# Loading the modulation matrix first, the small parameters from ScalarE's queue, and the front's projection weights through a pool of their own

## The chip, the cores and the metric

The kernel runs on one core of a Trainium2 chip. Its engines are TensorE (PE; PEld is its weight load), VectorE (DVE), ScalarE (ACT), GpSimd (POOL) and SyncE (SP). Each works through its own instructions in the order in which they stand. Copies between device memory and on-chip memory are issued by an engine's sequencer (SP in most cases, ACT and POOL in some) and carried by 16 DMA engines. The metric is the device time of one execution in microseconds.

## The reference

One layer of a hybrid backbone over 2048 latent tokens and 256 context tokens, all in 32-bit floats. What matters here is its beginning:

```python
silu_c, silu_cc = silu(c), silu(c_ctx)
mod_l = silu_c @ ada_w + ada_b              # 1024 -> 6 * 1024: shift, scale, gates
mod_c = silu_cc @ ada_w + ada_b
hl = rms_norm(x, norm_mix_pre) * (1 + scale_l) + shift_l
hc = rms_norm(ctx, norm_mix_pre) * (1 + scale_c) + shift_c
p = hl @ w_in, hc @ w_in                    # columns split among three mixers
...                                         # RWKV-7, gated delta net, RG-LRU in both directions
x = x + gate * rms_norm(concat(mixers) @ w_out)
x = x + gate * rms_norm(square(relu(h2 @ ffn_up)) @ ffn_down)
```

No product with `w_in` can start before scale and shift are known, and these need `c`, `c_ctx`, the first 2048 columns of `ada_w` (8 MB) and a part of `ada_b`.

## The kernel before

`body` runs four stages: `front`, `mixed`, `rest`, `ffn`. Only `front` is touched. Tokens go through it in nine pieces of 256, the context first.

- `K.__init__` makes constants on GpSimd and calls `params`. It loads 19 small vectors, row by row, into two tiles of 128 rows (`rawA`: c, c_ctx, ada_b and two norms; `rawB`: the rest) with 21 transfers from SP (lines 182 and 187), transposes each tile on TensorE and copies it to `parA`, `parB`.
- `ada_first` computes silu(c) as `cs` (two tanh on ScalarE into `csth`, four small VectorE steps), loads the 8 MB of `ada_w` as four tiles `adawt` of 2 MB (two transfers each, line 216) and multiplies: per tile 8 products (`adps`, recorded as 16 matmuls), a copy `adar`, four small transposes `adpt`, two additions. The result is `sc` and `sh`.
- `make_h` is a generator. It writes zeros between the pieces of the scratch tensor `ht` (`zf`, three transfers of 2048 runs of two or three numbers, line 295), loads a piece of x as two tiles `mhx`, takes sums of squares on ScalarE, runs `rms` (a chain of small VectorE steps), scales on GpSimd, then transposes (`mhps`), applies `sc` and `sh` (ScalarE for one half of the split numbers, VectorE for the other, in tiles `mhh`) and writes to `ht`, four transfers of 512 KB for a piece.
- `Proj` holds `w_in` as high and low parts (`whi`, `wlo`): `weight` loads 256 KB pieces into a staging buffer, ScalarE casts the high part, VectorE or GpSimd subtracts. The staging buffers are the six `hx` units, which later hold pieces read back from `ht` (four units a piece).
- `rwkv_sweep` multiplies piece by piece (`proj`) and does the RWKV preparation, and advances `make_h` beside it.

The order within each engine is set by a scheduler that goes by its own model of time when the program is built. Transfers issued by SP and ACT count on eight semaphores (DMAHW0 to 7) in turn. An issue waits until the transfer that used its semaphore before has landed, so eight at most are in flight from both engines together; and as each engine works in order, what stands behind a waiting issue waits too. Buffers given out again make their new writer wait for the last reader.

Of the kernel before, what the change touches and what calls it, by code (L numbers as in the profile page):

```python
# [7 lines left out]
F32 = mybir.dt.float32  # L8
# [4 lines left out]
PSUM = bass.MemoryType.PSUM  # L13
DRAM = bass.MemoryType.DRAM
ADD, SUB, MUL = ALU.add, ALU.subtract, ALU.mult

D = 1024
KD = 8
# [12 lines left out]
C_Z, C_BA, C_LX, C_LG, C_RW = 1152, 1536, 1560, 1816, 2072  # L31
# [44 lines left out]
class K:  # L76


    def __init__(self, tc, d, es):
        self.tc, self.nc, self.d = tc, tc.nc, d  # L80
        nc = self.nc
        self.V, self.A, self.G, self.PE, self.S = nc.vector, nc.scalar, nc.gpsimd, nc.tensor, nc.sync
        self.const = es.enter_context(tc.tile_pool(name="const", bufs=1))
        self.cols = {}
        self.tables = self.section = None
        self.inside = []
        c = self.const
        self.ident = c.tile([128, 128], F32, name="ident")
        self.G.memset(self.ident, 0.0)
        self.G.affine_select(self.ident, self.ident, pattern=[[-1, 128]], compare_op=ALU.not_equal,  # L90
                             fill=1.0, base=0, channel_multiplier=1)
        self.ones2 = c.tile([128, 128], F32, name="ones2")
        self.G.memset(self.ones2, 0.0)
        self.G.memset(self.ones2[0:64, 0:64], 1.0)
        self.G.memset(self.ones2[64:128, 64:128], 1.0)
        self.ones = c.tile([128, 128], F32, name="ones")
        self.G.memset(self.ones, 1.0)
        self.params()

    def col(self, v):  # L100

# [61 lines left out]

    def params(self):

        d, S, tc = self.d, self.S, self.tc
        rowsA = [("c", 8), ("c_ctx", 8), ("ada_b", 48), ("norm_mix_pre", 8), ("norm_ffn_pre", 8)]
        rowsB = [("gdn_conv", 36), ("lru_conv", 8), ("lru_conv_b", 2), ("lru_ba", 4), ("lru_bx", 4),
                 ("lru_lambda", 4), ("rwkv_mu", 12), ("rwkv_w0", 6), ("rwkv_a0", 6), ("rwkv_k_k", 3),
                 ("rwkv_k_a", 3), ("rwkv_r_k", 3), ("rwkv_gn_w", 3), ("rwkv_gn_b", 3)]  # L170
        self.pc = {}
        with tc.tile_pool(name="par", bufs=1) as p, tc.tile_pool(name="parp", bufs=2, space=PSUM) as pp:
            for nm, rows in (("A", rowsA), ("B", rowsB)):
                n = sum(r for _, r in rows) + (1 if nm == "B" else 0)
                raw = p.tile([128, 128], F32, name=f"raw{nm}")
                self.G.memset(raw, 0.0)
                o = 0
                place = {}
                for k, r in rows:
                    src = d[k]  # L180
                    names = " ".join(f"a{i}" for i in range(len(src.shape)))
                    S.dma_start(out=raw[o:o + r, :], in_=src.rearrange(f"{names} -> ({names})").rearrange("(r q) -> r q", q=128))
                    place[k] = (o, r)
                    o += r
                if nm == "B":
                    for hh in range(2):
                        S.dma_start(out=raw[o:o + 1, 64 * hh:64 * hh + 64], in_=d["gdn_norm"])
                    place["gdn_norm"] = (o, 1)
                ps = pp.tile([128, 128], F32, name=f"parps{nm}")
                self.PE.transpose(ps, raw, self.ident)  # L190
                t = self.const.tile([128, 128], F32, name=f"par{nm}")
                self.V.tensor_copy(t, ps)
                for k, (o, r) in place.items():
                    self.pc[k] = t[:, o:o + r]

def ada_first(k, pp, tag):

    c = k.const  # L200
    k.cs = c.tile([128, 2, KD], F32, name="cs")
    th = c.tile([128, 2, KD], F32, name="csth")
    for j, nm in enumerate(("c", "c_ctx")):
        k.act(th[:, j], k.pc[nm], AF.Tanh, scale=0.5)
        k.ts(k.V, th[:, j], th[:, j], 0.5, MUL, 0.5, ADD)
        k.tt(k.V, k.cs[:, j], th[:, j], k.pc[nm], MUL)
    k.sc = c.tile([128, 2, KD], F32, name="sc")
    k.sh = c.tile([128, 2, KD], F32, name="sh")
    with k.tc.tile_pool(name="adaw", bufs=4, reuse_waits="tile") as p:
        for j, o in ((1, k.sc), (0, k.sh)):  # L210
            for hf in range(2):
                w = p.tile([128, KD, 512], F32, name="adawt")
                c0 = j * D + hf * 512
                for q in range(2):
                    s = slice(4 * q, 4 * q + 4)
                    k.S.dma_start(out=w[:, s, :], in_=k.d["ada_w"][0, 512 * q:512 * q + 512, c0:c0 + 512].rearrange(
                        "(k p) f -> p k f", p=128))
                ps = pp.tile([128, 512], F32, name="adps", tag=tag)
                for kk in range(KD):
                    k.mm(ps[0:2, :], k.cs[:, :, kk], w[:, kk, :], kk == 0, kk == KD - 1)  # L220
                row = p.tile([2, 512], F32, name="adar", bufs=1)
                k.V.tensor_copy(row, ps[0:2, :])
                ps = pp.tile([128, 4, 2], F32, name="adpt", tag=tag)
                for m in range(4):
                    k.PE.transpose(ps[:, m, :], row[:, 128 * m:128 * m + 128], k.ident[0:2, 0:2])
                m = slice(4 * hf, 4 * hf + 4)
                for i in range(2):
                    k.tt(k.V, o[:, i, m], ps[:, :, i], k.pc["ada_b"][:, 8 * j + m.start:8 * j + m.stop], ADD)
    for i in range(2):
        k.stt(k.sc[:, i], k.sc[:, i], 1.0, k.pc["norm_mix_pre"], ADD, MUL)  # L230

# [55 lines left out]
def make_h(k, w, pp, tag):  # L287


    d = k.d  # L290
# [3 lines left out]
    for o, n in ((0, 2), (258, 3), (2309, 3)):  # L294
        k.S.dma_start(out=ht[:, :, o:o + n], in_=zf[:, :, 0:n])

    def load(p):
        xt = []
        for i in range(2):
            t = w.tile([128, D], F32, name="mhx", bufs=2)  # L300
            src = d["ctx"][0, 128 * i:128 * i + 128, :] if p == 0 else \
                d["x"][0, 256 * (p - 1) + 128 * i:256 * (p - 1) + 128 * i + 128, :]
            k.S.dma_start(out=t, in_=src)
            xt.append(t)
        return xt

    xt = load(H_ORDER[0])
    yield
    for n, p in enumerate(H_ORDER):
        j = 1 if p == 0 else 0  # L310
# [7 lines left out]
        for i, x in enumerate(xt):  # L318
            o = poff(p) + 2 + 128 * i
            for q in range(2):  # L320
                ps = pp.tile([128, 4, 128], F32, name="mhps", tag=tag)
                for a in range(4):
                    kk = 4 * q + a
# [16 lines left out]
def split(k, e, src, raw, hi, lo):  # L340

    k.S.dma_start(out=raw, in_=src)
    k.A.copy(hi, raw)  # L343
    k.tt(e, lo, raw, hi, SUB)
    return hi, lo


class Proj:
# [6 lines left out]
        self.pp = es.enter_context(tc.tile_pool(name=tag + "p", bufs=psb, space=PSUM, side=side))  # L355
        self.nw = 0

    def weight(self, i, c0, m):

        k = self.k  # L360
        self.hi[i], self.lo[i] = [self.w.tile([128, KD, m], F32R, name=f"w{x}{i}") for x in ("hi", "lo")]
        n = 2 * self.u
        for q in range(0, KD, n):
            s = slice(q, q + n)
            split(k, (k.V, k.G)[i % 2], k.d["w_in"][0, 128 * q:128 * (q + n), c0:c0 + m].rearrange("(k p) f -> p k f", p=128),
                  self.unit().bitcast(F32).rearrange("p k a t -> p (k a t)")[:, 0:n * m].rearrange("p (k f) -> p k f", f=m),
                  self.hi[i][:, s, :], self.lo[i][:, s, :])

# [1 line left out]

        return self.hp.tile([128, self.u, 2, PW], F32R, name="hx")

    def weights(self, cols):

        self.hi, self.lo, self.coming = {}, {}, ()
        for i, c in enumerate(cols):
            self.weight(i, *c)

    def passes(self, sets):

# [13 lines left out]
    def load(self, p):  # L394

        out = []
        o = poff(p)
        for q in range(0, KD, self.u):
            x = self.unit()
            self.k.S.dma_start(out=x.bitcast(F32).rearrange("p k a t -> p (k a) t"),  # L400
                               in_=self.k.d["ht"][:, q:q + self.u, :, o:o + PW].rearrange("p k a t -> p (k a) t"))
            out.append(x)
        return out
# [353 lines left out]
RW_TILES = [9, 10, 11, 3, 4, 5, 6, 7, 8, 0, 1, 2]  # L757


def rwkv_sweep(k, pj, pss, beside):  # L760


    d, tc, V, A, G = k.d, k.tc, k.V, k.A, k.G
# [1 line left out]
    with ExitStack() as es:  # L765
# [37 lines left out]
                k.stt(out, ps[:, 0:256], hmu[:, f:f + 1], out, MUL, ADD)  # L803
                k.stt(out, ps[:, 2:258], hmu[:, f:f + 1], out, MUL, ADD)

        ahead = pj.load(RW_ORDER[0])
        for i, p in enumerate(RW_ORDER):
            h = ahead
            if i + 1 < NP:
# [97 lines left out]
def front(k):  # L907

    with ExitStack() as es:
        pj = Proj(k, es, "r", psb=3, u=2, hb=6, side="left")  # L910
        pss = es.enter_context(k.tc.tile_pool(name="rss", bufs=3, space=PSUM))
        parts = make_h(k, es.enter_context(k.tc.tile_pool(name="mh", bufs=1, side="right")), pss, "rps")
        next(parts)
        ada_first(k, pss, "rps")
        for _ in range(9):
            next(parts)
        pj.weights([(C_RW + 128 * f, 128) for f in RW_TILES])
        rwkv_sweep(k, pj, pss, parts)


def softplus(k, p, x, n, m, tag):
# [945 lines left out]
```

## Time and profile before

| | us |
|---|---|
| median of 3 runs (lowest, highest) | 4212.22 (4210.96, 4213.60) |
| the profiled execution's own time | 4211.31 |
| its span on the core | 4209.5 |
| TensorE busy | 3570.4 (85%) |
| VectorE, ScalarE, GpSimd busy | 2391.7, 1480.0, 1387.2 |

The profile's page gives averages over stages with different limits, so for a change at the start the views of the first 110 us are read: the timeline of each engine (with the idle time before an instruction and what ended it), the busy times and DMA rates by stretch, and the waits. PEclk is the granted clock of TensorE (0.5 is 1.2 GHz, 1.0 is 2.4 GHz).

### The profile page before, as it was taken

The page shows a single profiled execution, that of the slowest core. Times are in us where ns is not written, and L with a number is a line of the kernel's source. Part 1 is how long each engine was busy: PE and PEld are TensorE (multiplying, and loading weights), DVE is VectorE, ACT ScalarE, POOL GpSimd, SP SyncE. Part 2 cuts the span into 40 slices and gives each one's busy share as a digit, 9 for nine tenths or more (in the row PEclk, how much of TensorE's full clock was granted, in tenths as well). Part 3 has the DMA queues.
Part 4 walks back from the last instruction along what each step waited for, and adds up shares of the span by engine and source line. Part 5 has one row for each costly group of instructions (what it writes and reads, how often), then busy time and mean ns, then how long its engine had stood idle before and what let it go on. Part 6 is the DMA issues. An engine that isn't in the chain of part 4 may idle for free. (4 is left out here: it accounts for less than half of the span.)

```text
span 4209.5 us, 75439 instructions
## 1 busy us (share of the span) xinstructions
PE 3570.4 (85%) x29914; PEld 2983.6 (71%) x29914; DVE 2391.7 (57%) x4533; ACT 1480.0 (35%) x2983; POOL 1387.2 (33%) x1373
## 2 busy tenths in 40 slices
PE   4767798688878876788787589989999999999998
PEld 1646678587767766677665467768888887888886
DVE  3456576885686562359979975643333346333334
ACT  2343344344445432223454444532222222211212
POOL 2123123233434432225456545322232214212212
PEclk8868899688979877688897679999999999999999
DMA  8554443656657755375665555631212123111112
GB/s 209 114 134 138 118 150 136 187 155 182 199 175 219 224 170 164 111 225 167 189 210 160 158 174 177 204 116 46 66 57 62 56 73 126 55 46 46 53 43 85
DMA packets 568885, 566.07 MB, mean 134 GB/s; under 512 B 42179, under 2 KB 521044, under 8 KB 568532
## 3 DMA queue, kind: packets, MB, share of 16 engines
q1 hardware_dynamic: 554708, 538.16, 42.9%
q0 software_dynamic: 5120, 16.78, 1.4%
q10 hardware_dynamic: 8704, 6.29, 0.5%
q8 instruction: 237, 3.88, 0.4%
q14 instruction: 116, 0.95, 0.1%
HBM read 425.96 MB, written 145.77 MB: 136 GB/s over the span
## 5 line engine op out<-in xcount | busy, mean ns | idle before, releaser
L162 PE MATMUL proj<-hx,whi 128*128 128x258 f32 (+2 forms) x4080 | 865.4, 309 | 99.5 <-DMA hx<-ht 40.9
L162 PEld LDWEIGHTS proj<-hx,whi 128*128 128x128 f32 x4080 | 684.9, 203 | 145.7 <-issue 66.9
L162 PE MATMUL proj<-hx,wlo 128*128 128x258 f32 (+2 forms) x2040 | 616.6, 303 | 0.0
L136 DVE TENSOR_TENSOR facc<-facc,fdn 128x512 f32<-128x512 f32 x480 | 326.1, 686 | 401.3 <-PE fdn L162 401.3
L162 PEld LDWEIGHTS proj<-hx,wlo 128*128 128x128 f32 x2040 | 413.2, 203 | 11.3 <-issue 6.8
L162 PE MATMUL fup<-fhh,uhi 128*128 128x512 f32 x1024 | 403.9, 395 | 3.8 <-ACT fhh L343 3.8
L162 PE MATMUL fup<-fhl,uhi 128*128 128x512 f32 x1024 | 402.9, 394 | 3.5 <-DVE fhl L136 3.3
L162 PE MATMUL fdn<-dhi,ah 128*128 128x512 f32 x1024 | 399.3, 391 | 4.1 <-ACT ah L1767 2.0
L162 PE MATMUL fup<-fhh,ulo 128*128 128x512 f32 x1024 | 402.8, 393 | 0.0
L162 PE MATMUL fdn<-dlo,ah 128*128 128x512 f32 x1024 | 399.2, 390 | 0.2 <-POOL dlo L136 0.2
L162 PE MATMUL fdn<-dhi,al 128*128 128x512 f32 x1024 | 395.0, 390 | 0.9 <-DVE al L136 0.9
L343 ACT CAST dhi<-draw 128x1024 fp32r<-128x1024 f32 x64 | 67.1, 1048 | 578.9 <-PE fdn L162 514.4
L136 POOL TENSOR_TENSOR dlo<-draw,dhi 128x1024 fp32r<-128x1024 f32 x32 | 77.5, 2421 | 565.0 <-ACT dhi L343 565.0
L136 POOL TENSOR_TENSOR fq<-fr 128x512 f32<-128x512 f32 x128 | 151.7, 1186 | 325.1 <-ACT fr L114 324.4
L162 PEld LDWEIGHTS fup<-fhl,uhi 128*128 128x128 f32 x1024 | 192.5, 188 | 49.1 <-DVE fhl L136 5.0
L162 PEld LDWEIGHTS fup<-fhh,uhi 128*128 128x128 f32 x1024 | 192.5, 188 | 48.8 <-ACT fhh L343 4.9
L162 PEld LDWEIGHTS fdn<-dhi,ah 128*128 128x128 f32 x1024 | 192.1, 188 | 48.6 <-DVE facc L136 3.3
L162 PEld LDWEIGHTS fup<-fhh,ulo 128*128 128x128 f32 x1024 | 192.3, 188 | 44.4
L136 DVE TENSOR_TENSOR al<-fq,ah 128x512 fp32r<-128x512 f32 x128 | 93.6, 732 | 227.3 <-ACT ah L1767 226.9
L162 PEld LDWEIGHTS fdn<-dhi,al 128*128 128x128 f32 x1024 | 192.2, 188 | 42.3 <-DVE al L136 1.3
L162 PEld LDWEIGHTS fdn<-dlo,ah 128*128 128x128 f32 x1024 | 192.3, 188 | 41.8 <-POOL dlo L136 0.6
L144 DVE SCALAR_TENSOR_TENSOR gy<-proj,parB,gy 128x256 f32<-128x256 f32 x243 | 115.1, 479 | 136.2 <-ACT gy L114 132.9
(365 smaller groups left out, 7207.4 us busy)
## 6 DMA issues: line engine op xcount, KB each, us to landing
hx<-ht SPq DMA_DIRECT2D x144, 520.0 KB
hx<-ht SPq DMA_DIRECT2D x36, 1040.0 KB
uraw<-in_ffn_up_dram SPq DMA_DIRECT2D x64, 512.0 KB
draw<-in_ffn_down_dram SPq DMA_DIRECT2D x64, 512.0 KB
pk<-pk SPq DMA_DIRECT2D x18, 1536.0 KB
pk<-pk SPq DMA_DIRECT2D x36, 768.0 KB
ht<-mhh SPq DMA_DIRECT2D x36, 512.0 KB
pb<-pk SPq DMA_DIRECT2D x36, 384.0 KB
```

Source lines behind the costliest of these rows:

```text
L136: return e.tensor_tensor(out=out, in0=a, in1=b, op=op)
L144: return self.V.scalar_tensor_tensor(out=out, in0=a, scalar=s, in1=b, op0=op0, op1=op1)
L162: self.last = self.PE.matmul(out, l, r, start=start, stop=stop).ins
L343: k.A.copy(hi, raw)
```

## The change

`params` is called later and issues from ScalarE's queue, as does the load of the first piece; the eight transfers of `ada_w` are issued by SP ahead of all else; the `w_in` staging gets 24 buffers of its own, which reuse the memory of the `ada_w` tiles; and the loads of `w_in` and of the first piece of `ht` are asked for after the first piece of h.

```diff
     # K.__init__
-        self.params()
     # params
-        d, S, tc = self.d, self.S, self.tc
+        d, S, tc = self.d, self.A, self.tc
-        with ... tc.tile_pool(name="parp", bufs=2, space=PSUM) as pp:
+        with ... tc.tile_pool(name="parp", bufs=1, space=PSUM) as pp:
+ADA_FIRST = ((1, 0), (1, 1), (0, 0), (0, 1))
+def ada_load(k, p):          # the loads, taken out of ada_first as they were
+    for j, hf in ADA_FIRST:
+        w = p.tile([128, KD, 512], F32, name="adawt")
...
     # make_h
-    def load(p):
+    def load(p, q=k.S):
-            k.S.dma_start(out=t, in_=src)
+            q.dma_start(out=t, in_=src)
-    xt = load(H_ORDER[0])
+    xt = load(H_ORDER[0], k.A)
     # Proj.weight
-                  self.unit().bitcast(F32)...
+                  raw.tile([128, n, m], F32, name="wraw") if raw else
+                  self.unit().bitcast(F32)...
     # rwkv_sweep: the first piece is handed in
-        ahead = pj.load(RW_ORDER[0])
     # front
-        next(parts)
-        ada_first(k, pss, "rps")
-        for _ in range(9):
-            next(parts)
-        pj.weights([(C_RW + 128 * f, 128) for f in RW_TILES])
-        rwkv_sweep(k, pj, pss, parts)
+        with k.tc.tile_pool(name="adaw", bufs=4, reuse_waits="tile") as p:
+            ws = ada_load(k, p)
+            k.params()
+            parts = make_h(k, mh, pss, "rps")
+            next(parts)
+            ada_first(k, p, ws, pss, "rps")
+        with k.tc.tile_pool(name="wst", bufs=2 * len(RW_TILES), reuse_waits="tile") as p:
+            for _ in range(3):
+                next(parts)
+            first = pj.load(RW_ORDER[0])
+            pj.weights([(C_RW + 128 * f, 128) for f in RW_TILES], p)
+            for _ in range(6):
+                next(parts)
+        rwkv_sweep(k, pj, pss, parts, first)
```

How ScalarE's instructions stand at the start: before, it has no transfers, and the tanh into `csth` is its fourth instruction.

```order
L129 ACT_TABLE_LOAD
L114 ACTIVATE mhh,mhs<-mhx 128x1024 [waits DMAHW0_49]
L114 ACTIVATE mhh,mhs<-mhx 128x1024 [waits DMAHW1_49]
L114 ACT_TABLE_LOAD
L114 ACTIVATE csth<-parA 128x8 [waits DVE_49]
```

In the changed kernel the same engine issues 23 transfers first; these are the last of them and what follows (each names the semaphore on which it waits).

```order
L181 DMA rawB<-in_rwkv_k_a_dram 3x128 [waits DMAHW3_49]
L181 DMA rawB<-in_rwkv_r_k_dram 3x128 [waits DMAHW4_49]
L181 DMA rawB<-in_rwkv_gn_w_dram 3x128 [waits DMAHW5_49]
L181 DMA rawB<-in_rwkv_gn_b_dram 3x128 [waits DMAHW6_49]
L186 DMA rawB<-in_gdn_norm_dram 1x64 [waits DMAHW7_49]
L186 DMA rawB<-in_gdn_norm_dram 1x64 [waits DMAHW0_49]
L312 DMA mhx<-in_ctx_dram 128x1024 [waits DMAHW1_49]
L113 ACT_TABLE_LOAD
L113 ACTIVATE mhh,mhs<-mhx 128x1024
L128 ACT_TABLE_LOAD
L113 ACT_TABLE_LOAD
L113 ACTIVATE csth<-parA 128x8 [waits DVE_49]
```

The tanh now stands behind all parameter loads, both context tiles and three table loads.

SP's transfers at the start, before: the parameters, the zeros, `ada_w`, `w_in`.

```order
L182 DMA rawB<-in_rwkv_gn_b_dram 3x128
L187 DMA rawB<-in_gdn_norm_dram 1x64 x2
L295 DMA ht<-zf 2048x1x2
L295 DMA ht<-zf 2048x1x3 x2
L216 DMA adawt<-in_ada_w_dram 128x4x512 x8
L342 DMA hx<-in_w_in_dram 128x4x128 x23
```

And in the changed kernel, from the sixth transfer of `ada_w` on, with the semaphores.

```order
L208 DMA adawt<-in_ada_w_dram 128x4x512 [waits DMAHW2_49]
L208 DMA adawt<-in_ada_w_dram 128x4x512 [waits DMAHW4_49]
L208 DMA adawt<-in_ada_w_dram 128x4x512 [waits DMAHW6_49]
L304 DMA ht<-zf 2048x1x2 [waits DMAHW0_49,Pool_49]
L304 DMA ht<-zf 2048x1x3 [waits DMAHW2_49]
L304 DMA ht<-zf 2048x1x3 [waits DMAHW4_49]
L351 DMA wraw<-in_w_in_dram 128x4x128 [waits DMAHW2_49,DMAHW1_49,PE_49]
L351 DMA wraw<-in_w_in_dram 128x4x128 [waits DMAHW3_49,PE_49]
L312 DMA mhx<-in_x_dram 128x1024 [waits DMAHW4_49,PE_49,Pool_49]
L351 DMA wraw<-in_w_in_dram 128x4x128 [waits DMAHW5_49]
```

The zeros moved behind `ada_w`; their semaphores 0, 2 and 4 are those that ScalarE's later parameter loads wait on (`rwkv_r_k`, number 4, above). The third `w_in` transfer stands behind a load of x that waits for TensorE.

SP further on, before: the first piece goes out to `ht` and comes back as `hx` with `w_in` long issued.

```order
L333 DMA ht<-mhh 128x8x128
L303 DMA mhx<-in_x_dram 128x1024
L333 DMA ht<-mhh 128x8x128 x2
L400 DMA hx<-ht 128x4x260 x2
L333 DMA ht<-mhh 128x8x128
L400 DMA hx<-ht 128x4x260 x2
```

In the changed kernel the same stretch, from the third transfer of `w_in` on.

```order
L351 DMA wraw<-in_w_in_dram 128x4x128 x10
L342 DMA ht<-mhh 128x8x128
L312 DMA mhx<-in_x_dram 128x1024
L342 DMA ht<-mhh 128x8x128
L351 DMA wraw<-in_w_in_dram 128x4x128 x12
L342 DMA ht<-mhh 128x8x128 x2
L410 DMA hx<-ht 128x4x260 x2
```

Ten and then twelve of the 24 transfers of `w_in` now stand between the load of x and the last writes of the first piece.

## Rows read from the trace of the kernel before

**Rows 1.** TensorE, timeline: start us, us, engine line op, tiles, [idle before <-releaser]

```profile
26.70 9.41 PE L162 MATMUL adps<-adawt,cs 128*2 128x512 f32 x16 [14.83 <-DMA adawt<-in_ada_w_dram]
...
45.03 0.41 PE L225 MATMUL adpt<-ident,adar 2*128 2x2 f32 x4 [0.77 <-DVE adar L222]
...
63.66 0.41 PE L225 MATMUL adpt<-ident,adar 2*128 2x2 f32 x4 [3.13 <-DVE adar L222]
...
95.09 0.77 PE L162 MATMUL proj<-hx,whi 128*128 128x258 f32 x2 [22.18 <-DMA hx<-ht]
...
104.11 0.51 PE L162 MATMUL proj<-hx,whi 128*128 128x258 f32 x2 [1.49 <-DMA hx<-ht]
```

**Rows 2.** SP's timeline

```profile
0.81 0.87 SPq L303 DMA_DIRECT2D mhx<-in_ctx_dram  x2
...
4.49 0.27 SPq L182 DMA_DIRECT2D rawB<-in_lru_conv_dram  x1
...
9.67 0.54 SPq L187 DMA_DIRECT2D rawB<-in_gdn_norm_dram  x2
10.33 2.78 SPq L295 DMA_DIRECT2D ht<-zf  x3
13.16 20.05 SPq L216 DMA_DIRECT2D adawt<-in_ada_w_dram  x8
33.26 12.09 SPq L342 DMA_DIRECT2D hx<-in_w_in_dram  x6
```

**Rows 3.** by stretch: PE, PEld, DVE, ACT, POOL busy, PEclk, DMA share, GB/s

```profile
16.00:17.00 1.00, 0.00 (x0) 0.00 (x0) 0.00 (x0) 0.00 (x0) 0.00 (x0) 1.00 2.47 7
...
19.00:20.00 1.00, 0.00 (x0) 0.00 (x0) 0.00 (x0) 0.00 (x0) 0.00 (x0) 1.00 1.09 62
...
24.00:25.00 1.00, 0.00 (x0) 0.00 (x0) 0.00 (x0) 0.00 (x0) 0.00 (x0) 1.00 0.71 184
25.00:26.00 1.00, 0.00 (x0) 0.00 (x0) 0.00 (x0) 0.00 (x0) 0.00 (x0) 1.00 1.03 397
```

**Rows 4.** the same view, while ada_w and while w_in are loaded

```profile
36.00:40.00 4.00, 3.23 (x12) 0.92 (x12) 0.91 (x3) 0.00 (x0) 0.00 (x0) 1.00 1.05 409
...
52.00:56.00 4.00, 3.23 (x11) 0.83 (x11) 2.34 (x5) 1.89 (x4) 2.39 (x3) 1.00 1.00 260
```

**Rows 5.** by stretch, later in the front

```profile
150.00:200.00 50.00, 33.93 (x253) 33.57 (x253) 20.48 (x63) 17.57 (x35) 5.70 (x2) 0.79 0.63 135
```

**Rows 6.** TensorE's waits, 95 to 600 us; columns: total us, times, longest

```profile
PE rps L162 <- POOL kd L136: 28.1, 4, 13.9
PE proj L162 <- ACT mhh L114: 23.7, 3, 19.1
```

**Rows 7.** ScalarE's timeline at the start

```profile
4.50 1.06 ACT L114 ACTIVATE mhh<-mhx 128x1024 f32<-128x1024 f32 x1 [2.41 <-DMA mhx<-in_ctx_dram]
...
7.00 1.28 ACT L114 ACT_TABLE_LOAD   x1
8.29 0.31 ACT L114 ACTIVATE csth<-parA 128x8 f32<-128x8 f32 x2
```

**Rows 8.** transfers by kind, 0 to 130 us: count, KB each

```profile
adawt<-in_ada_w_dram SPq DMA_DIRECT2D x8, 1024.0 KB
hx<-in_w_in_dram SPq DMA_DIRECT2D x24, 256.0 KB
ht<-mhh SPq DMA_DIRECT2D x8, 512.0 KB
```

**Rows 9.** SP's waits, 0 to 130 us

```profile
SPq L182 <- DMA mhx<-in_ctx_dram: 1.7, 2, 1.0
```

**Rows 10.** the rms chain before the second piece: VectorE's first step

```profile
92.04 0.15 DVE L141 TENSOR_SCALAR rms<-mhs 128x1 f32<-128x1 f32 x1 [3.88 <-ACT mhh L114]
```

**Rows 11.** and GpSimd, which waits for its end

```profile
94.86 5.67 POOL L140 TENSOR_SCALAR mhx<-mhx,rms 128x1024 f32<-128x1024 f32 x2 [22.97 <-DVE rms L144]
```

**Rows 12.** SP, the first piece out to ht and back

```profile
90.85 0.91 SPq L400 DMA_DIRECT2D hx<-ht  x2
```

More of the change, by code (lines that the diff above doesn't have):

```diff
@@ L171, in params @@
         self.pc = {}
-        with tc.tile_pool(name="par", bufs=1) as p, tc.tile_pool(name="parp", bufs=2, space=PSUM) as pp:
+        with tc.tile_pool(name="par", bufs=1) as p, tc.tile_pool(name="parp", bufs=1, space=PSUM) as pp:
             for nm, rows in (("A", rowsA), ("B", rowsB)):
@@ L194, in params, with ada_first @@
                     self.pc[k] = t[:, o:o + r]
-def ada_first(k, pp, tag):
+ADA_FIRST = ((1, 0), (1, 1), (0, 0), (0, 1))
+def ada_load(k, p):
+    ws = []
+    for j, hf in ADA_FIRST:
+        w = p.tile([128, KD, 512], F32, name="adawt")
+        c0 = j * D + hf * 512
+        for q in range(2):
+            s = slice(4 * q, 4 * q + 4)
+            k.S.dma_start(out=w[:, s, :], in_=k.d["ada_w"][0, 512 * q:512 * q + 512, c0:c0 + 512].rearrange(
+                "(k p) f -> p k f", p=128))
+        ws.append(w)
+    return ws
+def ada_first(k, p, ws, pp, tag):
     c = k.const
@@ L208, in ada_first @@
     k.sh = c.tile([128, 2, KD], F32, name="sh")
[L209 to L228, printed above, removed]
+    for (j, hf), w in zip(ADA_FIRST, ws):
+        o = k.sc if j else k.sh
+        ps = pp.tile([128, 512], F32, name="adps", tag=tag)
+        for kk in range(KD):
+            k.mm(ps[0:2, :], k.cs[:, :, kk], w[:, kk, :], kk == 0, kk == KD - 1)
+        row = p.tile([2, 512], F32, name="adar", bufs=1)
+        k.V.tensor_copy(row, ps[0:2, :])
+        ps = pp.tile([128, 4, 2], F32, name="adpt", tag=tag)
+        for m in range(4):
+            k.PE.transpose(ps[:, m, :], row[:, 128 * m:128 * m + 128], k.ident[0:2, 0:2])
+        m = slice(4 * hf, 4 * hf + 4)
+        for i in range(2):
+            k.tt(k.V, o[:, i, m], ps[:, :, i], k.pc["ada_b"][:, 8 * j + m.start:8 * j + m.stop], ADD)
     for i in range(2):
@@ L356, in __init__, with weight @@
         self.nw = 0
-    def weight(self, i, c0, m):
+    def weight(self, i, c0, m, raw=None):
         k = self.k
@@ L371, in unit, with weights @@
         return self.hp.tile([128, self.u, 2, PW], F32R, name="hx")
-    def weights(self, cols):
+    def weights(self, cols, raw=None):
         self.hi, self.lo, self.coming = {}, {}, ()
         for i, c in enumerate(cols):
-            self.weight(i, *c)
+            self.weight(i, *c, raw)
     def passes(self, sets):
@@ L757, with rwkv_sweep @@
 RW_TILES = [9, 10, 11, 3, 4, 5, 6, 7, 8, 0, 1, 2]
-def rwkv_sweep(k, pj, pss, beside):
+def rwkv_sweep(k, pj, pss, beside, ahead):
     d, tc, V, A, G = k.d, k.tc, k.V, k.A, k.G
@@ L911, in front @@
         pss = es.enter_context(k.tc.tile_pool(name="rss", bufs=3, space=PSUM))
-        parts = make_h(k, es.enter_context(k.tc.tile_pool(name="mh", bufs=1, side="right")), pss, "rps")
-        next(parts)
-        ada_first(k, pss, "rps")
-        for _ in range(9):
-            next(parts)
-        pj.weights([(C_RW + 128 * f, 128) for f in RW_TILES])
-        rwkv_sweep(k, pj, pss, parts)
+        mh = es.enter_context(k.tc.tile_pool(name="mh", bufs=1, side="right"))
+        with k.tc.tile_pool(name="adaw", bufs=4, reuse_waits="tile") as p:
+            ws = ada_load(k, p)
+            k.params()
+            parts = make_h(k, mh, pss, "rps")
+            next(parts)
+            ada_first(k, p, ws, pss, "rps")
[7 more added lines that the diff above has]
+        rwkv_sweep(k, pj, pss, parts, first)
 def softplus(k, p, x, n, m, tag):
```

## The prediction

> **What bounds the kernel now.** The change touches only the first stage, so I read that stage in order of time. TensorE's timeline comes first: it idles until 26.70 us, when the first tile of `ada_w` is there, works through four tiles until 64.07, and idles again until 95.09, when the first piece has come back from `ht` [rows 1]. Next, SP's timeline says why `ada_w` is late: ahead of it stand the parameters, until 10.21, and three transfers of zeros; the 8 MB go out from 13.16 [rows 2]. The view by stretch prices the zeros: from about 11 to 25 us the DMA engines are busy and move almost nothing, 7 GB/s at 16 us and still 184 at 24, and only from 25 on do they reach 397 [rows 3]. While `ada_w` runs alone it is 409 GB/s; while `w_in` runs it is 260 at a full DMA share [rows 4]. The reader should see a chain: zeros, `ada_w`, TensorE's four tiles, the first piece out and back. After it TensorE is busy 33.9 of 50 us and waits for the other engines [rows 5, 6].
>
> **The change, part by part.**
>
> *`ada_w` first.* Its issue moves from 13.16 to 0.81 us [rows 2]. With the flow starting near 2 us (an estimate from that issue and the first use of a context tile at 4.50 [rows 7]), 8.39 MB [rows 8] and one context tile of 0.52 MB take 8.91 / 0.409 = 21.8 us [rows 4] and are in by 24. Taken alone that would let TensorE start long before 26.70.
>
> *The zeros behind it.* They are issued as soon as the fifth to seventh transfers land, and stand in the same queue behind the eighth. Before, `ada_w` got nothing done until the zeros were through [rows 3], so I take the queue as first in, first out here too: 24 + 13 = 37 us. Lower bound for the 13 is 8 (the first bytes of `ada_w` pass at 19 us, 62 GB/s), upper 14.
>
> *Parameters on ScalarE's queue.* Here the change works against itself. An issue waits for the transfer that had its semaphore before: SP's load of `lru_conv` stood until 4.49, held by a context tile [rows 2, 9]. In the new order `rwkv_r_k` waits on semaphore 4, last used by the third transfer of zeros, hence until 37. Behind it ScalarE still has six issues at 0.3 us each [rows 2], the second context tile's among them: 1.9, to 39. Then a table load, 1.28, and the sum of squares, 1.06 + 0.19 for its readout, rounded to 1.2 [rows 7]. VectorE must run the whole `rms` chain before it reaches the copy of `parA`, on which the tanh waits: 94.86 − 92.04 = 2.8 [rows 10, 11], during which two more table loads pass on ScalarE. Copy 0.3 (an estimate, two small steps), tanh 0.3 [rows 7], and four small steps for `cs` that I put at 0.9 (0.15 each [rows 10] with gaps): 6.8 together. The first product starts at 39 + 6.8 = 46, not 26.70: 19 us later. Before, `cs` had long been ready and its cost was nothing, because the wait for `ada_w` hid it; that cover is gone.
>
> No row shows ScalarE waiting at an issue of its own. The Trainium skill ("DMA: Bandwidth & Descriptors", Anatomy of one DMA) states that the DMA engines never wait on semaphores; the wait sits on the issuing sequencer before dispatch. By that rule ScalarE stands still as SP does; were it otherwise, the first rival below would hold.
>
> *TensorE's four tiles.* From 26.70 to 64.07 is 37.4 us, of which the last small transposes lost 3.13 − 0.77 = 2.4 to a VectorE that was held by the `w_in` splits [rows 1]. In the new kernel the splits come later, so 35.0. The transposes of `parB` slip in behind the first tile; their loads land about 2 us after 39 and the tile ends near 55, so that costs nothing. Modulation is done at 46 + 35 = 81 instead of 64.07: **+17**.
>
> *`w_in` behind the first piece.* Its first two transfers wait only for TensorE to be done with the tiles whose memory they reuse. The third stands on SP behind a load of x that waits for the context tile to be transposed, that is, until just after modulation. So 22 of 24 transfers, which before were hidden beside the four tiles (26 to 64 us), now share the next stretch with the first piece. From modulation to the first product of the sweep was 95.09 − 64.07 = 31.0 us [rows 1]. Now it must pass 22 × 0.262 MB of `w_in` and four writes of 0.524 MB at 260 GB/s, (5.77 + 2.10) / 0.260 = 30.2, and two loads of x, 1.05 / 0.409 = 2.6 [rows 4, 8]; then the reading back, 95.09 − 90.85 = 4.2 [rows 1, 12]. With 0.5 for the first transposes that is 37.5, or 6.5 more. The second half of the piece gives some back: it arrived 9.0 us after the first (104.11 [rows 1]), held by the last write; now that write is issued ahead of both, so it follows at once and the second half starts about 4 later than before. I take **+5**. Lower bound 0 (the loads pass beside ScalarE's and VectorE's work on the piece, which before also left the DMA idle at times), upper +9 (every write queued behind all of `w_in`).
>
> *The rest.* The own staging pool frees the `hx` units, on whose reuse SP waited before; this lay beside the four tiles and is worth nothing. The single buffer for the parameter transposes makes `parB` wait for the copy of `parA`, done long before. After about a sixth of TensorE's and a quarter of VectorE's instructions the order is the same as before, so there is no lasting reorder to price; swaps of stores and loads inside the sweep may move a few us either way.
>
> *Sum.* 17 + 5 = +22 us on the profiled execution's 4211.3 (span 4209.5) gives 4233; the median of the runs shown, 4212.2, is 0.9 above that execution, so nothing changes. I assume the delay passes down whole: behind the first product every wait is for an engine that works on the same pieces [rows 6], and nothing started earlier runs on its own.
>
> A rule that speaks against the whole idea: the Trainium skill ("DMA: Bandwidth & Descriptors", Issuing engines are not separate DMA queues) says that issuing from several engines saves only the sequencer's issue time. SP's parameter issues end at 10.21 [rows 2], so by it the split could save at most some 9 us of issuing, and the trace agrees that the zeros, not the issues, fill the time from 11 to 25.
>
> **Rivals.**
>
> *ScalarE is not held (faster).* If all the semaphores were free in time, 23 issues at 0.3 us would end near 8; plus 6.8 the first product starts at 15, TensorE paces the tiles, modulation ends at 50, 14 early; less the 6.5 for `w_in`: −8, 4203. For it: the early transfers are tiny, and `ada_w` is in time for each tile (2 MB in 5 us against (63.66 − 2.4 − 45.03) / 2 = 8.1 of TensorE a tile [rows 1]). Against: the order of the semaphores, and rows 9. It decides if the last zeros landed before about 18 us; from some 27 on it is a loss.
>
> *The delay is swallowed (same).* TensorE's longest wait after the start, 19.1 us, is for `mhh`, work of `make_h` [rows 6]. If that chain had slack, the 22 us could vanish there: 4212. Against: `make_h` starts later by the same amount, since its second piece stands behind the first.
>
> *Only part is lost.* If the zeros pass beside `ada_w` instead of behind it, say by 28 us, the first product starts at 37, modulation ends at 72, and with +5 for `w_in`, or nothing, the total is +8 to +13: about 4222.
>
> **How the numbers follow.** Forecast 0.77; part lost 0.11; swallowed 0.05; not held 0.07. The forecast's own range takes the bounds: 13 − 5 and + 1 for the zeros, 0 to +9 for `w_in`, and 0.5 us instead of 0.3 an issue should ScalarE's cost more (an estimate without a row): +12 to +28, 4223 to 4240. The range for 8 in 10 reaches into the part-lost case and leaves some us for the sweep's swaps and for TensorE's clock, which in the front is granted at 0.79 on average over 50 us [rows 5]: 4215 to 4244. About 0.2% (8 us) is what a measurement tells from no change; slower by more than that: 0.87; same 0.06; faster 0.07.
>
> **What would show it.** Right: ScalarE's tanh into `csth` near 43 us, and its issue of `rwkv_r_k` held until 36 to 38; the zeros after `ada_w`, again with a busy DMA at a few GB/s; the first product at 46, the last small transposes near 81, a first `proj` at 115 to 120. Wrong: a first product before 30 us (the semaphores did not hold ScalarE), zeros through by 30 (the 13 was mis-sized), or a first `proj` at 117 with an end that is not late (the delay was swallowed).

## The result

| | before | changed |
|---|---|---|
| median of 6 runs (lowest, highest), us | 4212.55 (4209.85, 4215.61) | 4241.84 (4238.05, 4251.19) |
| profiled span, us | 4209.5 | 4249.5 |
| TensorE busy, us | 3570.4 | 3557.4 |

The changed kernel takes 1.0073 of the time before (95% interval 1.006 to 1.0085): 29 us slower. The forecast was 4233, in a range of 4215 to 4244. The profiled execution is the slowest of its six; a second profile of the same kernel, below, has a span of 4240.8, so where a size matters both are given.

TensorE's timeline of the changed kernel (start, duration, idle time before and its releaser), against [rows 1]:

```profile
43.21 8.44 PE L161 MATMUL adps<-adawt,cs 128*2 128x512 f32 x16 [30.68 <-DVE cs L135]
...
76.82 0.40 PE L234 MATMUL adpt<-ident,adar 2*128 2x2 f32 x4 [0.77 <-DVE adar L231]
...
119.87 0.77 PE L161 MATMUL proj<-hx,whi 128*128 128x258 f32 x2 [36.76 <-DMA hx<-ht]
...
756.98 1.08 PE L161 MATMUL rm<-pb 64*64 64x64 f32 x14 [0.76 <-PE rps L161]
...
2833.16 0.40 PE L161 MATMUL fdn<-dhi,ah 128*128 128x512 f32 x1
```

And two rows further down the same timeline before, for which nothing stood in the rows so far:

```profile
723.57 1.54 PE L162 MATMUL rm<-pb 64*64 64x64 f32 x24
...
2793.45 0.39 PE L162 MATMUL fdn<-dhi,ah 128*128 128x512 f32 x1
```

Read as delays: the first product comes 43.21 − 26.70 = 16.5 us later, and what it waited for is no longer `ada_w` but `cs`. Modulation is done at 77.22 instead of 64.07, +13.2. The first product of the sweep is +24.8. In the mixers (`rm`) it is +33, in the feed-forward (`fdn`) +40. So five sixths of the median's 29 us are there by the first `proj`; the rest grows later.

ScalarE's queue of the changed kernel, which answers to [rows 7]:

```profile
13.16 0.25 ACTq L181 DMA_DIRECT2D rawB<-in_lru_bx_dram  x1
25.67 0.27 ACTq L181 DMA_DIRECT2D rawB<-in_lru_lambda_dram  x1
...
33.05 0.25 ACTq L181 DMA_DIRECT2D rawB<-in_rwkv_k_k_dram  x1
...
34.77 0.25 ACTq L181 DMA_DIRECT2D rawB<-in_rwkv_r_k_dram  x1
...
36.31 0.36 ACTq L312 DMA_DIRECT2D mhx<-in_ctx_dram  x1
36.70 1.28 ACT L113 ACT_TABLE_LOAD   x1 [36.70 <-DMA rawB<-in_rwkv_gn_b_dram]
...
41.79 0.31 ACT L113 ACTIVATE csth<-parA 128x8 f32<-128x8 f32 x2
```

Each issue takes 0.3 us, yet the twelve behind `lru_bx` are out only at 36.7. The tanh on which everything depends needs only `parA`, whose loads were issued by 8.2; it stands behind parameters that it doesn't need.

The view by stretch of the changed kernel (busy times of five engines, clock, DMA share, GB/s), against [rows 3], and SP's timeline, against [rows 2, 12]:

```profile
22.00:24.00 2.00, 0.00 (x0) 0.00 (x0) 0.00 (x0) 0.00 (x0) 0.00 (x0) 1.00 1.05 409
24.00:26.00 2.00, 0.00 (x0) 0.00 (x0) 0.00 (x0) 0.00 (x0) 0.00 (x0) 1.00 1.06 195
26.00:28.00 2.00, 0.00 (x0) 0.00 (x0) 0.00 (x0) 0.00 (x0) 0.00 (x0) 1.00 0.77 17
...
30.00:32.00 2.00, 0.00 (x0) 0.00 (x0) 0.00 (x0) 0.00 (x0) 0.00 (x0) 1.00 0.66 5
```

```profile
0.81 14.96 SPq L208 DMA_DIRECT2D adawt<-in_ada_w_dram  x8
18.01 8.57 SPq L304 DMA_DIRECT2D ht<-zf  x3
...
78.71 7.13 SPq L351 DMA_DIRECT2D wraw<-in_w_in_dram  x10
85.95 0.58 SPq L342 DMA_DIRECT2D ht<-mhh  x1
...
88.68 0.38 SPq L342 DMA_DIRECT2D ht<-mhh  x1
89.11 15.52 SPq L351 DMA_DIRECT2D wraw<-in_w_in_dram  x12
104.73 6.08 SPq L342 DMA_DIRECT2D ht<-mhh  x2
111.72 1.00 SPq L410 DMA_DIRECT2D hx<-ht  x2
```

`ada_w` runs at 409 GB/s and is in by about 25; then the zeros run alone, at 5 to 17 GB/s from 26 to 32. `lru_lambda` goes out when the last of `ada_w` has landed, `rwkv_k_k` and `rwkv_r_k` as the zeros land, at 33 and 34.8. After modulation ten transfers of `w_in` stand ahead of the first piece's first write and twelve more ahead of its last two.

Of that second stretch, the two waits of ScalarE for the first piece's writes, before and then in the changed kernel, and two rows by stretch of the changed kernel:

```profile
78.79 0.46 ACT L114 ACTIVATE mhh<-mhps,sh,sc 128x128 fp32r<-128x128 f32 x1 [7.14 <-DMA ht<-mhh]
83.25 1.40 ACT L114 ACTIVATE mhh<-mhps,sh,sc 128x128 fp32r<-128x128 f32 x3 [2.13 <-DMA ht<-mhh]
```

```profile
94.87 0.46 ACT L113 ACTIVATE mhh<-mhps,sh,sc 128x128 fp32r<-128x128 f32 x1 [3.77 <-DMA ht<-mhh]
100.78 0.81 ACT L113 ACTIVATE mhh<-mhps,sh,sc 128x128 fp32r<-128x128 f32 x2 [3.57 <-DMA ht<-mhh]
```

```profile
92.00:96.00 4.00, 0.00 (x0) 0.00 (x0) 0.41 (x1) 0.65 (x2) 0.95 (x1) 0.50 1.11 205
96.00:100.00 4.00, 0.00 (x0) 0.00 (x0) 0.82 (x2) 0.73 (x2) 0.00 (x0) 0.50 1.18 185
```

From 92 to 100 the engines are nearly idle while the DMA is full: the two buffers `mhh` wait until the first piece's writes have passed behind `w_in`. ScalarE waits for these writes before as well. Counted from the end of modulation, though, it goes on at 14.7 and 19.2 us before, and at 17.6 and 23.6 us in the changed kernel.

### The profile page after: what moved, and what is told of

It is laid out like the page before. It is cut to its first block, busy times and chain, and to the rows that moved or that the text cites. A ratio compares the mean times of both kernels' runs of the same rounds, so it can differ in the third digit from the quotient of the medians.

```text
span 4249.5 us, 75409 instructions
## 1 busy us (share of the span) xinstructions
PE 3557.4 (84%) x29914; PEld 2971.5 (70%) x29914; DVE 2399.2 (56%) x4533; ACT 1478.5 (35%) x2982; POOL 1394.9 (33%) x1373
## 5 line engine op out<-in xcount | busy, mean ns | idle before, releaser
L161 PEld LDWEIGHTS fdn<-dlo,ah 128*128 128x128 f32 x1024 | 192.3, 188 | 41.7 <-POOL dlo L135 0.6
```

What stands on the lines that cost most here:

```text
L161: self.last = self.PE.matmul(out, l, r, start=start, stop=stop).ins
```

## The experiments

All compared with the kernel before on the same chip. The table holds three milestones of each profile in us: the first product with `ada_w`, the last small transposes `adpt`, with which modulation ends, and the first `proj`, which opens the sweep. Beside them stands the median against that of the kernel before.

| kernel | first product | last `adpt` | first `proj` | median − before | ratio (95%) |
|---|---|---|---|---|---|
| before | 26.70 | 63.66 | 95.09 | | |
| changed, again | 43.74 | 78.29 | 120.59 | +31.2 | 1.0070 (1.0054, 1.0087) |
| win_old | 47.67 | 87.14 | 114.36 | +26.0 | 1.0060 (1.0043, 1.0077) |
| params_pool | 25.56 | 59.68 | 102.46 | +24.8 | 1.0059 (1.0041, 1.0076) |
| params_sp | 11.30 | 49.40 | 91.48 | −11.0 | 0.9974 (0.9963, 0.9985) |
| after_zpool | 45.45 | 80.20 | 123.05 | +37.3 | 1.0088 (1.0073, 1.0104) |
| sp_win_old | 11.22 | 53.56 | 89.40 | 0.0 | 1.0001 (0.9990, 1.0012) |
| zeros_late | 15.49 | 60.84 | 93.17 | +21.8 | 1.0052 (1.0038, 1.0066) |
| sp_win_old_zpool | 16.36 | 55.63 | 89.74 | +19.5 | 1.0049 (1.0036, 1.0063) |
| half_loads | 43.50 | 77.55 | 119.84 | +5.1 | 1.0015 (1.0001, 1.0030) |
| half_splits | 43.59 | 78.34 | 119.73 | +33.9 | 1.0091 (1.0062, 1.0119) |

**The changed kernel again.** No edit.

> The changed kernel once more, unaltered, for a second profile. Theory A (the front's delay of 24.8 us at the first projection passes down whole, and what the first profile shows beyond it, a lag that grows to 40 us by the end, belongs to that one execution): 4238 to 4245 us, the first projection again near 119.9 us, a lag behind before at the end of 25 to 33 us. Rival B (the changed order inside the sweep costs 10 to 15 us more, always): the lag grows again from 24 to about 40 at the same places.

The delay is the same; the profile's span is 4240.8, so some 9 us of the first profile's 40 were its own. About 6 us beyond the first `proj`'s +25.5 remain.

**win_old: `w_in` as before.**

```diff
-            pj.weights([(C_RW + 128 * f, 128) for f in RW_TILES], p)
+        for _ in range(9): next(parts)
+        pj.weights([(C_RW + 128 * f, 128) for f in RW_TILES])   # through the hx units
```

> The changed kernel with w_in staged as before, through the hx units and not behind the first piece; ScalarE still issues the parameters. Theory A: first product as in the changed kernel, 43 us (41 to 46), modulation done at 77, then 31 us as before: first projection near 108, time 4222 to 4230. Rival C (the own pool behind the first piece is most of the loss): 4212 to 4218, since only 13 of 25 us of delay would remain and the sweep would swallow them.

ScalarE's queue here is the clearest picture of the hold:

```profile
19.52 0.25 ACTq L181 DMA_DIRECT2D rawB<-in_rwkv_k_a_dram  x1
38.91 0.25 ACTq L181 DMA_DIRECT2D rawB<-in_rwkv_r_k_dram  x1
```

All issues before it are through by 19.8; one stands 19 us, and all of ScalarE behind it. It waits here for a transfer of `w_in`, issued at 34.73, that uses the same semaphore ahead of it; so the first product comes 4.5 us later than in the changed kernel. The stretch from modulation (87.55) to the first `proj` falls to 26.8 us, from 42.65. But the tiles paid for it:

```profile
76.33 0.58 PE L234 MATMUL adpt<-ident,adar 2*128 2x2 f32 x4 [3.63 <-DVE adar L231]
```

Casts and subtractions of `w_in` beside the tiles held the last two by about 6 us together. So the time missed its expectation (4237, not 4222 to 4230): that `w_in` stands behind the piece costs 16 us of its stretch, and saves 10 of these ahead of it.

**params_pool: the parameters and the first piece from GpSimd.** `d, S, tc = self.d, self.G, self.tc`, and `load(H_ORDER[0], k.G)`.

> Parameters and the first piece issued by GpSimd, whose transfers count on other semaphores; ada_w first and w_in as in the changed kernel. Theory A: ScalarE is not held any more, first product at 15 us (11 to 19) instead of 43.2, modulation done near 50, first projection near 50 + 42.6 = 93, time 4206 to 4214, the same as before within 0.2%. Rival B (the order in the sweep, or rival C, the own pool of w_in with the loads behind the first piece, makes the loss): 4225 to 4240.

A miss: the hold on ScalarE is gone, its tanh runs at 15.58, and yet the first product starts at 25.56. VectorE's timeline says why:

```profile
23.98 0.29 DVE L191 COPY parB<-parpsB 128x128 f32<-128x128 f32 x1 [8.44 <-PE parpsB L189]
24.19 1.05 DVE L140 TENSOR_SCALAR csth<-csth 128x8 f32<-128x8 f32 x2
```

The steps for `cs` stood behind the copy of `parB`, which waits for the last parameter; GpSimd needs 0.5 us for each issue and waits for semaphores too (its last issue ends at 19.36). The same fault in another place: what is urgent behind what is not. Modulation gains 4 us by it, the first `proj` comes 7.4 later, and the median is 24.8 above before.

**params_sp: the parameters on SP, ahead of the zeros.** `d, S, tc = self.d, self.S, self.tc`, `load(H_ORDER[0])`, and `params()` called before `ada_load`; SP then issues them behind the second transfer of `ada_w`.

> The changed kernel with parameters and the first piece issued by SP again, beside the loads of ada_w and ahead of the zeros; w_in through its own pool behind the first piece. Theory A: first product at 11 us (9 to 14), modulation done near 46, first projection near 46 + 42.6 = 89, time 4202 to 4210, slightly faster than before. Rival C (the own pool is most of the loss): 4225 or more.

```profile
11.30 9.67 PE L161 MATMUL adps<-adawt,cs 128*2 128x512 f32 x16 [1.13 <-DMA rawB<-in_rwkv_k_k_dram]
...
49.40 0.40 PE L234 MATMUL adpt<-ident,adar 2*128 2x2 f32 x4 [4.02 <-DVE adar L231]
...
91.48 0.77 PE L161 MATMUL proj<-hx,whi 128*128 128x258 f32 x2 [35.17 <-DMA hx<-ht]
```

The edit that is left of the change, `ada_w` first, does what it is for: the first product 15 us earlier than before, 32 earlier than in the changed kernel. Of the 14 us at the last `adpt`, 10.7 are lost again in the stretch with `w_in`, 41.7 us long instead of 31.0. The kernel beats both (0.9974), but not by its front alone: 3.6 us at the first `proj`, 11 in the median.

**after_zpool: the zeros from GpSimd.** `k.G.dma_start(out=ht[:, :, o:o + n], in_=zf[:, :, 0:n])`.

> The changed kernel with one edit: the three transfers of zeros are issued by GpSimd, not by SP behind ada_w, so that no parameter load on ScalarE's queue shares a semaphore with them. Theory (the hold of ScalarE behind the zeros makes the first product late, and the zeros' 10 us are a wait of their own): ada_w is all in by 25 to 26 us as in the changed kernel, ScalarE's last issue falls near 29 instead of 36, the first product starts near 36 instead of 43 to 44, modulation ends near 70, the first proj comes near 112, and the time is 4232 to 4236. Rival A (the zeros cost the DMA engines 10 us whoever issues them): the last of ada_w lands near 35, ScalarE is held until then by it, the first product starts at 42 to 44, and the time stays at 4240 to 4245. Rival B (ScalarE is not held by semaphores at all, something else makes it late): its first product stays at 43 to 44 although ada_w is in by 26.

Rival A, and a little worse: the same kernel's GpSimd, SP and ScalarE, in this order.

```profile
2.72 3.56 POOL L304 DMA_DIRECT2D ht<-zf  x3
```

```profile
0.81 25.32 SPq L208 DMA_DIRECT2D adawt<-in_ada_w_dram  x8
```

```profile
8.95 0.66 ACTq L181 DMA_DIRECT2D rawB<-in_lru_conv_dram  x1
28.32 0.24 ACTq L181 DMA_DIRECT2D rawB<-in_lru_conv_b_dram  x1
```

The zeros take the same time beside `ada_w` as behind it: the eighth issue of `ada_w` ends at 26.1 instead of 15.8. ScalarE is now held by `ada_w` itself, from 9.6 to 28.3. That agrees with the Trainium skill ("DMA: Bandwidth & Descriptors", Issuing engines are not separate DMA queues), by which transfers from all engines share the same 16 DMA engines.

**zeros_late: the kernel before, with the zeros behind `ada_w`.** The loop over `zf` moves behind the first `yield` of `make_h`.

> The kernel before with one edit: the three transfers of zeros are issued by SP behind ada_w instead of ahead of it. Parameters and w_in as before. Theory (the zeros ahead of ada_w hold its first tile back by 10 to 13 us, and nothing else does): first product near 17 instead of 26.7, modulation done near 54, w_in starts 0 to 10 us later than before and its splits run beside the first piece, first proj at 86 to 91 instead of 95.1, time 4203 to 4208. Rival (the zeros cost the same wherever they stand, since w_in comes late by them and the first piece behind it): first product at 17, but first proj at 94 to 97, time 4210 to 4213.

```profile
15.49 9.12 PE L162 MATMUL adps<-adawt,cs 128*2 128x512 f32 x16 [3.60 <-DMA adawt<-in_ada_w_dram]
...
48.97 0.58 PE L225 MATMUL adpt<-ident,adar 2*128 2x2 f32 x4 [8.09 <-DVE adar L222]
...
93.17 0.77 PE L162 MATMUL proj<-hx,whi 128*128 128x258 f32 x2 [22.11 <-DMA hx<-ht]
```

The first product gains 11 us, the first `proj` 1.9, close to the rival's 94: with the zeros between `ada_w` and `w_in`, the splits of `w_in` come late and hold VectorE when a tile ends (8.09). The time missed both, 4235.86.

**sp_win_old: `ada_w` first, parameters on SP, `w_in` through the hx units ahead of the piece.**

> ada_w first on SP, with the parameters on SP behind its second transfer and the zeros behind its last (as in the run with the parameters on SP), but w_in staged through the hx units as in the kernel before, asked for ahead of the first piece. Theory (w_in behind the first piece costs some 11 us of the stretch from modulation to the first proj, since the first piece's writes queue behind it): first product at 11, modulation done at 50 to 56 (the splits run beside the last tiles), the stretch to the first proj 27 to 31 us instead of 42, first proj at 80 to 86, time 4190 to 4197. Rival (the w_in bytes cost the same wherever they pass): first proj at 91 as with the own pool, time 4200.

The stretch is 35.3 us (54.14 to 89.40), between the two expectations, and 2 us are gained over params_sp at the first `proj`; yet against the kernel before, params_sp gained 11 us and this one none. **sp_win_old_zpool** takes its zeros from GpSimd as well.

> As the run with ada_w first and parameters and w_in on SP as before, but the zeros are issued by GpSimd early. If the zeros are a wait of their own that passes beside ada_w: first product at 11 to 14, w_in issued from about 28 us, modulation done at 48 to 52, first proj at 76 to 83, time 4185 to 4195. If they take the DMA engines' time wherever they are: ada_w is later by up to 10 us, first product at 18 to 24, modulation done at 55 to 60, first proj at 84 to 90, time 4196 to 4206.

The first product, at 16.36, lies between the two expectations; the end of modulation (56.0) and the first `proj` (89.74) fall within the second, by which the zeros take the DMA engines' time wherever they are. They cost 5 us at the start against sp_win_old. The first `proj` comes 5.3 us earlier than before; the time, 4233.5, is 19.5 above it and misses both expectations.

**half_loads and half_splits** were to say what makes the stretch with `w_in` long, the transfers or the splits. The first loads only one half of each column block and takes the second from the same tile, so that it multiplies with wrong weights; the second sets every second `wlo` to zero.

```diff
+            if raw and q:               # half_loads
+                k.A.copy(hi, t); k.tt(e, lo, t, hi, SUB)
+                continue
+            if raw and q:               # half_splits
+                k.G.memset(lo.bitcast(F32), 0.0); k.S.dma_start(out=t, in_=src); k.A.copy(hi, t)
+                continue
```

> The changed kernel with every second of the 24 transfers of w_in in the front left out: the second half of each column block is taken from the same staging tile as the first, so that all casts and subtractions stay (the projection is computed with wrong weights). Up to modulation nothing changes (first product at 43 to 45, modulation done at 77 to 80). Theory (the stretch from modulation to the first proj, 42 to 43 us instead of 31, is long because the first piece's writes to ht stand in the queue behind w_in's transfers, so that ScalarE and VectorE, with two buffers for mhh, wait for them): the stretch falls to 32 to 36 us, first proj at 110 to 115. Rival (it is long because VectorE, GpSimd and ScalarE have the splits of w_in to do in it): it stays at 40 to 43, first proj at 118 to 121.

> The changed kernel with all 24 transfers and all casts of w_in, but with every second subtraction for wlo left out (that half is set to zero by GpSimd instead; the projection lacks these corrections): VectorE and GpSimd have six instead of twelve of them, some 1.6 us each, in the stretch. Theory (the queue): the stretch from modulation to the first proj stays at 38 to 43 us. Rival (the splits): it falls by 6 to 10 us, to 33 to 36, first proj at 111 to 114.

The second came as the queue theory has it: 41.0 us, with VectorE idle until ScalarE's wait for the first write ends.

```profile
96.48 0.41 DVE L140 TENSOR_SCALAR mhh<-mhps,sc,sh 128x128 f32<-128x128 f32 x1 [6.26 <-ACT mhh L113]
```

The first contradicts that theory as stated, and came as its rival has it: half the transfers, and still 41.9 us. There the scheduler put eight splits in one run ahead of the piece's last steps on VectorE:

```profile
90.34 12.37 DVE L135 TENSOR_TENSOR wlo<-wraw,whi 128x512 fp32r<-128x512 f32 x8
102.63 0.72 DVE L140 TENSOR_SCALAR mhh<-mhps,sc,sh 128x128 f32<-128x128 f32 x2
```

and the two last writes left at 107.63 instead of 104.73. So two things can fill this stretch, and with half of either gone the other still fills it. In half_loads the DMA stood still from 100 to 108, and the piece's way out and back, from 107.63 to the first `proj`, still took 12.2 us.

## Why the prediction was right, and where its sizes were off

*Zeros behind `ada_w`.* Right in kind. From the end of `ada_w` to the landing of the last zeros 9 to 10 us passed (25 to 34.8), not 13; the bounds were 8 and 14. The 13 ran to 25 us in the kernel before, but there `ada_w` was already passing slowly in the last six of them, at 62 to 184 GB/s [rows 3].

*ScalarE held at its issues.* Right, and the step that decided: `rwkv_r_k` was forecast to stand until 37 (36 to 38) and stood until 34.77. From there to the first product 8.4 us passed (43.21), forecast 9 (1.9 + 6.8 with rounding). params_sp, with no transfer on ScalarE's queue, started at 11.30; win_old shows the wait at one issue. The rival that ScalarE is not held fell with these. The rival that only a part is lost needed the zeros through by 28, and the one that the delay is swallowed an end that is not late; neither came.

*Four tiles.* 34.0 us (43.21 to 77.22), forecast 35.0. The sum at this point is +13, forecast +17: 2.2 us of the difference are the zeros, 1.0 the tiles, the rest ScalarE's steps and rounding.

*`w_in` behind the first piece.* This is the term that was mis-sized: +11.6 at the first `proj` against +6.5 worked out for that point, and +5 taken. SP's loads of the piece were issued 34.5 us after modulation; from the rates 33.3 had been expected. The two agree within 1.2 us, but that does not show the sum of bytes to be the cause: half_loads, with half of these transfers, issued its loads 35.2 us after modulation (77.95 to 113.14). What clearly failed is the reading back: 8.15 us (111.72 to 119.87) instead of the 4.2 taken from [rows 1, 12]. It shows in the rates. Changed kernel, then before, both while the first two `hx` are read:

```profile
114.00:115.00 1.00, 0.00 (x0) 0.00 (x0) 1.00 (x11) 0.07 (x1) 0.11 (x1) 0.50 1.11 116
115.00:116.00 1.00, 0.00 (x0) 0.00 (x0) 1.00 (x12) 0.00 (x0) 0.00 (x0) 0.50 0.92 158
116.00:117.00 1.00, 0.00 (x0) 0.00 (x0) 0.97 (x9) 0.00 (x0) 0.12 (x1) 0.50 1.00 102
```

```profile
93.00:94.00 1.00, 0.00 (x0) 0.00 (x0) 0.86 (x10) 0.18 (x2) 0.00 (x0) 0.50 1.03 338
94.00:95.00 1.00, 0.00 (x0) 0.00 (x0) 0.94 (x8) 0.00 (x0) 0.14 (x1) 0.50 1.00 315
```

In the changed kernel the last write stands just ahead of the reading, in the place that the prediction booked as a gain. The gain came too (the second half followed without a wait), but some 4 us of slow reading ate it. That the stretch is longer with `w_in` in it is shown by win_old (26.8 us against 42.65); which share the queue and VectorE have in general is not separated by the two runs made for it. In the changed kernel's own trace the first write goes out 8.7 us after modulation, as before (72.75, 85.95); then the landings of two writes take more time, and the third write is issued 0.1 us behind the last of the twelve transfers (104.63, 104.73). So 7.7 us are lost on this way until the reading is issued, and 3.9 more in the reading.

*The rest passes down whole.* Not quite: the medians are 29 to 31 us above before, the first `proj` 24.8 and 25.5. Some 5 us more are lost behind it, where the prediction allowed only "a few us either way". In the second profile the delay is 30.2 us at the first `rm` and 31.2 at the first `fdn`, so they are lost in the sweep, where one place shows a step of that size. SP's timeline there, before and then in the second profile of the changed kernel, with what ScalarE waited for:

```profile
490.89 5.00 SPq L471 DMA_DIRECT2D vr<-vr  x4
...
500.05 0.55 SPq L904 DMA_DIRECT2D bv<-bv  x1
```

```profile
522.35 8.00 SPq L481 DMA_DIRECT2D vr<-vr  x4
530.39 2.02 SPq L913 DMA_DIRECT2D bv<-bv  x1
...
537.61 0.92 ACT L838 COPY g<-rps 128x256 f32<-128x256 f32 x3 [8.54 <-DMA bv<-bv]
```

In the kernel before, the four `vr` are out by 495.9, the store of `pk` goes behind them (495.94), and `bv` 2 us after that. In the changed kernel `pk` goes ahead of `vr` (521.70), and `bv` is issued only when the last `vr` is out. ScalarE's `g`, and TensorE's products behind it, come 30.6 us later than before (507.01 and 537.61); TensorE's last products ahead of them (`rps<-kd,ork`, 493.68 and 517.70) had come 24.0 later. The first profile shows the same step, from 27.0 to 33.6. win_old and half_loads have these `vr` ahead of `pk`, as before, and lose nothing at this place (22.5 on both sides; 24.6 and 24.5). It is one of the "swaps of stores and loads inside the sweep" of the prediction. That it costs the 6 us is read from the order and the times; no run changes it alone.

The prediction was right in its mechanism, but that the time lay in the range, 2 us below its upper end, is in part luck. At the first `proj` it had worked out 17 + 6.5 = +23.5, and +24.8 came, since 3.8 us too much ahead of modulation and 5.1 too little behind it nearly cancel.

The other runs show how little the front's milestones fix the end: zeros_late and sp_win_old_zpool are ahead of before at the first `proj` by 1.9 and 5.3 us and end 22 and 20 us behind; half_loads is 24.7 behind there and 5 at the end. In the changed kernel and win_old VectorE's instructions stand in the order of the kernel before from about 880 us on; in all the other runs they differ up to about 2700 us or later, since the scheduler plans anew from other start times. So their medians against each other say little about the front, and the params_sp gain beyond its front's 3.6 us is not to be credited to the front either: at the first `rm` that kernel is 2.6 us behind before, and at the first `fdn` 12.2 ahead.

## What to carry to other kernels

A queue that is moved to a compute engine brings its waits along: before issuing transfers from ScalarE, ask which earlier transfer each issue will wait for, and what that engine has to do behind it. Loading the big operand first is worth 15 us at the first product here when the small ones stay on SP, ahead of the slow zeros (zeros_late has 11 of the 15 by moving the zeros alone); but look at the next shared stage at once, for most of it was given back there. A gain or loss of a few us in a first stage is judged by its milestones, as the rest of the program is planned anew.

## What the chip showed that was not expected

- Three transfers of 2048 runs of 8 or 12 bytes keep the DMA engines busy for some 7 us (25 to 32) at 5 to 17 GB/s, and the last has landed 9 to 10 us after `ada_w`. Another queue did not hide them: with the zeros at the front, issued by GpSimd, the last issue of `ada_w` came 10 us later. The Trainium skill ("DMA: Bandwidth & Descriptors", Specifications) gives 512 bytes as the least size for full rate. The trace agrees as to runs of a few bytes; but `w_in`, in runs of 512 bytes, moved at 345 GB/s at a full DMA share (84 to 88 us of the changed kernel), and `ada_w`, in runs of 2 KB, at 409.
- Two 512 KB writes back to back, with the reading of the same data right behind: in half_loads, with nothing else in flight, the second write moved at 135 to 148 GB/s at a full DMA share (111 to 114 us), and the reading behind it at 95 to 176 (115 to 118 us). Before, with over 3 us between the write's data and the reading, the reading ran at 315 to 338. Why was not tried.
